# Four gate or up pieces at a time, a shared bank for the eighth chunk, and 8 KB runs of down weights

## The chip, the cores and the metric

The kernel runs on one core of a Trainium2 chip. The metric is the time of one execution on the device, in microseconds (us); the median of three runs stands for a kernel. The profile is of one execution. In its rows PE is TensorE's matmuls, PEld its loads of weights, DVE is VectorE, ACT ScalarE, POOL GpSimd, and SPq the queue of SyncE, which issues nearly all DMAs.

## The reference

One encoder block on 528 tokens (16 meta tokens and 512 inputs) of width 1024: RMSNorm, an input projection, differential attention beside a gated short convolution, an output projection, and then a layer of 16 experts, after which the meta tokens are dropped and a last RMSNorm follows. The experts are what this change touches. Each expert picks the 66 tokens with the highest affinity to it:

```
aff = softmax(hs @ w_router)                 # hs: normed hidden state, 528 x 1024
g, idx = top_k(aff.T, 66)                    # per expert
xg = hs[idx]                                 # 16 x 66 x 1024
a = xg @ w_gate ; u = xg @ w_up              # 66 x 2048 for each expert
y = (silu(a) * u) @ w_down                   # 66 x 1024
out = zeros.at[idx].add(y * g)               # back to the tokens
```

All weights are float32, 8 MB each for gate, up and down of one expert, so that the layer reads 402.7 MB (384 MiB) of them.

## The kernel before

The experts' weights come in pieces of 1 MiB. A gate or up piece has 256 of the 1024 input rows (two blocks of 128) and 1024 of the 2048 hidden columns; there are 16 of them for an expert: for each half h of the hidden columns four of gate (into the bank tile G) and then four of up (into U). A down piece has 256 of the 2048 hidden rows and all 1024 columns; there are 8. All go into one ring of 20 buffers (`raw`). The list `tasks` holds them in the order of use, `pump` (L752) issues a DMA on SyncE's queue for the next of them as soon as the ring's next buffer is free, and `nextw` pumps and hands the oldest piece to the matmuls.

The program of the expert layer is written out by hand in one loop over the experts (`manual_schedule`), and each engine runs its part in that order. For expert e TensorE does:

- a gate or up piece: 32 products (`prod`, L941) of a 128x64 block of weights, loaded, with the 66 gathered tokens X as what moves; float32 makes two matmuls and two loads of each, so a piece has 64 matmuls and 64 loads in the trace;
- after every second such piece, the one-hot product of the expert e-2 (`to_tokens`, L998: 128 tokens by 512 columns, two matmuls into the bank T, added into `acc` by VectorE, L999), and then one down piece of the expert e-1 (`down_piece`, L968 and L970: 24 matmuls of 32 columns into `y`);
- twice an expert, four transposes for the next expert's X (`turn_x`, L953, into T as well).

After four pieces of a half, ScalarE takes Silu of G into H, or VectorE multiplies H by U. `down_rows` reads y at the end of an expert. [...] Expert 0 has gate and up pieces alone, and expert 1 no one-hot products. The last expert's eight down pieces are used in a loop of their own behind the layer (tile `ys`), and there the work is followed by the sums, the last norm and the output.

Of the kernel before, what the change touches and what calls it, by code (L numbers as in the profile page):

```python
# [10 lines left out]
F32 = mybir.dt.float32  # L11
# [8 lines left out]
P = 128  # L20
D = 1024
DC = D // P
# [5 lines left out]
NE = 16  # L28
CAP = 66
# [25 lines left out]
def block_kernel(ctx: ExitStack, tc: tile.TileContext, x, meta, mix_g, w_in, conv_w, lq1, lk1, lq2,  # L55
                 lk2, sub_g, w_out, ffn_g, w_router, w_gate, w_up, w_down, fin_g, rope, out):
    nc = tc.nc
# [18 lines left out]
    def two(ap):  # L76
# [28 lines left out]
    rows = [(meta, NMETA, 0), (x[0, 0:128], 128, 16), (x[0, 128:256], 128, 144), (x[0, 256:384], 128, 272),  # L105
            (x[0, 384:496], 112, 400), (x[0, 496:512], NMETA, 512)]
# [17 lines left out]
    ident = const.tile([P, P], F32, name="ident")  # L124
# [103 lines left out]
    HS = (slice(0, HALF), slice(HALF, L))  # L228
# [353 lines left out]
    last = [Outs(0, c, None) for c in range(0, D, 256)]  # L582
# [132 lines left out]
    def moe_raw():  # L715
        i = moe_n[0] % NRAW
        moe_n[0] += 1
        for n, p in rings:
            if i < n:
                return p.tile([P, 2048], F32, name="raw", tag="raw")  # L720
            i -= n

    tasks = []
    def gate_up(e):
        return [w[0, e, k * 256:(k + 1) * 256, h * 1024:(h + 1) * 1024].rearrange("(c p) f -> p c f", p=P)
                for h in range(2) for w in (w_gate, w_up) for k in range(4)]

    def down(e):

        for d in range(8):  # L730
            rows, cols = slice(d * 256, (d + 1) * 256), slice(0, D)
            if e == NE - 1:
                rows, cols = slice(d % 4 * 512, (d % 4 + 1) * 512), slice(d // 4 * 512, (d // 4 + 1) * 512)
            yield w_down[0, e, rows, cols].rearrange("(c p) f -> p c f", p=P)


    for e in range(NE):
        dn = down(e - 1) if e else None
        for i, t in enumerate(gate_up(e)):
            tasks.append(t)  # L740
            if e and i % 2:
                tasks.append(next(dn))
    tasks.extend(down(NE - 1))
    queue = []

    def pump(n, eng=nc.sync):
        while len(queue) < n and tasks:
            t = moe_raw()
            a = tasks.pop(0)
            v = t.rearrange("p (c f) -> p c f", c=a.shape[1])  # L750
            if tasks:
                eng.dma_start(v, a)  # L752
            else:
                for k in range(2):
                    eng.dma_start(v[:, 2 * k:2 * k + 2], a[:, 2 * k:2 * k + 2])
            queue.append(t)

    pump(RING[0])


# [87 lines left out]
    for t in range(NT):  # L848
        if t % 2 == 0:
            hn2 = ring2.tile([P, 2048], F32, name="raw", tag="raw")  # L850
        n = P if t < 4 else NMETA
# [10 lines left out]
    for t in range(NT):  # L862
        n = P if t < 4 else NMETA
# [34 lines left out]
    def gather(e):  # L898
        xg = xgp.tile([CAP, D], F32, name="xg", tag="xg")
        nc.gpsimd.indirect_dma_start(out=xg, out_offset=None, in_=hn2_d,  # L900
                                     in_offset=bass.IndirectOffsetOnAxis(ap=idxT[:CAP, e:e + 1], axis=0))
        return xg

    xg = gather(0)
# [5 lines left out]
    last = const.tile([P, 2], F32, name="last")  # L910
# [14 lines left out]
    ps2 = psm.enter_context(tc.tile_pool(name="ps2", bufs=1, space=PSUM, reuse_waits="tile"))  # L925
    NF = DFF // P
    HS = [wk.tile([P, NF, CAP], F32, name=f"H{i}") for i in range(2)]
# [3 lines left out]
    def banks(tag, n):  # L931
        return ps2.tile([P, n, 512], F32, name=tag, tag=tag, bufs=1)

    def nextw():
        pump(NRAW)
        return queue.pop(0)

    def prod(out, w, c0, x, first, last):

        for q in range(2):  # L940
            nc.tensor.matmul(out[64 * q:64 * q + 64], w[:, c0 + 64 * q:c0 + 64 * q + 64], x, start=first, stop=last,  # L941
                             skip_group_check=True)

    def at(t, i):
        return t[:, i // 4, i % 4 * CAP:(i % 4 + 1) * CAP]

    def four(t, k):
        return t[:, k, :4 * CAP].rearrange("p (c n) -> p c n", n=CAP)

    def turn_x(X, xg, k):  # L950
        t = banks("T", 1)
        for i in range(4):
            nc.tensor.transpose(at(t, i), xg[:, (4 * k + i) * P:(4 * k + i + 1) * P], ident[:CAP, :CAP])  # L953
        nc.vector.tensor_tensor(X[:, 4 * k:4 * k + 4], four(t, 0),
                                gffn[:, 4 * k:4 * k + 4, None].to_broadcast([P, 4, CAP]), op=ALU.mult)

    def new_x():
        return wk.tile([P, DC, CAP], F32, name="X", tag="X", bufs=2)

    def down_piece(y, H, d):  # L960


        w = nextw()
        for r in range(3):
            ob, ci = ((0, 0), (0, 1), (1, 0))[r]
            o = ci * 1024 + ob * 512
            for g in range(3):
                nc.tensor.matmul(y[32 * g:32 * g + 32, ob], H[:, 2 * d + ci, GR[g]:GR[g] + 32], w[:, o:o + 512],  # L968
                                 start=d == 0 and r != 1, stop=d == 7 and r != 0, skip_group_check=True)
            nc.tensor.matmul(y[96:128, r], H[:, 2 * d + 1, GR[r]:GR[r] + 32], w[:, 1536:2048], start=d == 0, stop=d == 7,  # L970
                             skip_group_check=True)

    def down_rows(y, e):

        gate = at96[:96, NE + e:NE + e + 1]
        yh = wk.tile([96, D], FR, name="yh", tag="yh")
        yl = wk.tile([96, D], FR, name="yl", tag="yl")
        tmp = wk.tile([96, 512], F32, name="tmp", tag="tmp")
        a, b = slice(0, 512), slice(512, D)
        nc.scalar.activation(yh[:, a], y[:96, 0], AF.Copy, scale=gate)  # L980
        nc.vector.scalar_tensor_tensor(yl[:, a], y[:96, 0], gate, f32(yh[:, a]), op0=ALU.mult, op1=ALU.subtract)
        for g in range(3):
            gs = slice(32 * g, 32 * g + 32)
            nc.scalar.activation(tmp[gs], y[96:128, g], AF.Copy, scale=at96[gs, NE + e:NE + e + 1])
        nc.vector.scalar_tensor_tensor(tmp, y[:96, 1], gate, tmp, op0=ALU.mult, op1=ALU.add)
        nc.scalar.copy(yh[:, b], tmp)
        nc.vector.tensor_tensor(yl[:, b], tmp, f32(yh[:, b]), op=ALU.subtract)  # L987
        oh = wk.tile([96, 512], FR, name="oh", tag="oh")
        nc.gpsimd.tensor_scalar(oh, tok, at96[:96, e:e + 1], None, op0=ALU.is_equal)  # L989
        return oh, yh, yl  # L990

    def to_tokens(po, rows, d):

        oh, yh, yl = rows
        hf, t = divmod(d, 4)
        hfs = slice(hf * 512, (hf + 1) * 512)
        for n, b in enumerate((yh, yl)):
            nc.tensor.matmul(po, oh[:, t * P:(t + 1) * P], b[:, hfs], start=n == 0, stop=n == 1)  # L998
        nc.vector.tensor_tensor(acc[:, t, hfs], acc[:, t, hfs], po, op=ALU.add)  # L999
# [3 lines left out]
    X = new_x()  # L1003
    for k in range(2):
        turn_x(X, xg, k)
    xg = gather(1)
    rows = None
    for e in range(NE):
        H = HS[e % 2]
        y = banks("y", 3) if e else None  # L1010
        i = 0
        for h in range(2):
            for n in range(2):
                t = banks("GU"[n], 2)
                for k in range(4):
                    w = nextw()
                    for ci in range(2):
                        c = 2 * k + ci
                        for j in range(8):
                            prod(at(t, j), w, ci * 1024 + j * P, X[:, c], c == 0 and j % 4 == 0, c == DC - 1)  # L1020
                    if i % 2 and rows is not None:
                        to_tokens(banks("T", 1)[:, 0], rows, i // 2)
                    if i % 2 and e:
                        down_piece(y, HS[(e - 1) % 2], i // 2)
                    i += 1
                    if i in (10, 12) and e + 1 < NE:
                        if i == 10:
                            Xn = new_x()
                        turn_x(Xn, xg, i // 2 - 5)
                        if i == 12 and e + 2 < NE:  # L1030
                            xg = gather(e + 2)
                for k in range(2):
                    dst = H[:, 8 * h + 4 * k:8 * h + 4 * k + 4]
                    src = four(t, k)
                    if n == 0:
                        nc.scalar.activation(dst, src, AF.Silu)  # L1036
                    else:
                        nc.vector.tensor_tensor(dst, dst, src, op=ALU.mult)  # L1038
        if e:
            rows = down_rows(y, e - 1)  # L1040
        X = Xn
# [23 lines left out]
    for i in range(8):  # L1065
        w = nextw()
        hf, d = divmod(i, 4)
        for ci in range(4):
            f = 4 * d + ci
# [90 lines left out]
```

## Time and profile before

| | us |
|---|---|
| median of 3 runs (1379.19 to 1382.37) | 1381.4 |
| the profiled execution | 1379.79 |
| its span in the trace | 1378.0 |
| experts 0 to 15, from the first gate matmul to the last matmul of y | 978.1 (353.5 to 1331.6) |
| from there to the end of the span | 46.4 |

The span is what lies between the first and the last instruction; 1.8 us of the execution lie outside it. The profiled execution is 1.6 us under the median. [...] Some 71% of the span is the expert layer.

### The profile page before, as it was taken

The numbers are of one execution on the slowest core, as the hardware profiler recorded it, in microseconds if no ns is written. First come the engines' busy times: TensorE is split into PE (matmuls) and PEld (weight loads), VectorE is DVE, ScalarE is ACT, GpSimd is POOL, SyncE is SP. The second block draws the span as 40 slices with busy tenths as digits, with TensorE's granted clock in tenths as the row PEclk, the third lists the DMA queues.
The fourth block names the chain that finished last, engine by engine and source line by source line (L and its number), as shares of the span: only waits on it lengthen the run. The fifth ranks groups of instructions, "written<-read, shape, count | busy, mean of one in ns | idle before, by whom it ended". The sixth has DMA issues, their size and how long they took to land.

```text
span 1378.0 us, 47059 instructions
## 1 busy us (share of the span) xinstructions
PE 1256.9 (91%) x22308; PEld 927.0 (67%) x22308; DVE 393.1 (29%) x668; ACT 231.2 (17%) x431; POOL 174.9 (13%) x139
## 2 busy tenths in 40 slices
PE   7888889994679999999999999999999999999986
PEld 6677879994666666666666666666666666666654
DVE  5876776545000111112111112111111111111115
ACT  4455444322000101011010101001010101001012
POOL 2734441331100000000000000000000000000002
PEclk8999999996899999999999999999999999999998
DMA  7311211294899999999999999999999999999992
GB/s 207 92 31 31 62 32 62 93 384 167 320 352 408 396 395 407 391 407 396 406 397 404 385 391 397 393 400 388 403 382 397 400 385 404 380 405 398 407 362 94
DMA packets 142881, 434.49 MB, mean 315 GB/s; under 512 B 13200, under 2 KB 37776, under 8 KB 142688
## 3 DMA queue, kind: packets, MB, share of 16 engines
q1 hardware_dynamic: 139936, 423.49, 80.4%
q0 software_dynamic: 2752, 8.00, 1.9%
q8 instruction: 174, 2.85, 0.8%
q14 instruction: 19, 0.16, 0.0%
HBM read 427.19 MB, written 4.26 MB: 313 GB/s over the span
## 4 chain that ended last, share of the span: by engine, by line
PE 71%; DMA 12%; DVE 7%; issue 4%; ACT 3%; POOL 2%; SPq 0%; POOLq 0%; DVEq 0%; ACTq 0%
PE y L968 19%; PE G L941 16%; PE U L941 15%; DMA raw<-in_w_gate 6%; DMA raw<-in_w_up 6%; PE T L998 5%; PE pj L274 4%; PE pj L304 3%; PE ys L941 1%; ACT qsw L365 1%; PE pj L344 1%; PE sc L430 1%; PE T L953 1%; ACT p L441 1%; PE sc L792 1%
## 5 line engine op out<-in xcount | busy, mean ns | idle before, releaser
L968 PE MATMUL y<-raw,H 128*32 128x512 f32 x2160 | 337.1, 596 | 2.0 <-issue 2.0
L970 PE MATMUL y<-raw,H 128*32 128x512 f32 x720 | 332.2, 596 | 0.0
L941 PEld LDWEIGHTS U<-X,raw 128*64 128x64 f32 x8192 | 250.2, 138 | 65.0 <-issue 46.8
L941 PEld LDWEIGHTS G<-X,raw 128*64 128x64 f32 x8192 | 250.5, 139 | 58.4 <-issue 50.1
L941 PE MATMUL U<-X,raw 128*64 128x66 f32 x8192 | 263.0, 224 | 21.0 <-issue 14.9
L941 PE MATMUL G<-X,raw 128*64 128x66 f32 x8192 | 262.9, 224 | 17.4 <-issue 15.6
L999 DVE TENSOR_TENSOR acc<-acc,T 128x512 f32<-128x512 f32 x112 | 76.9, 687 | 599.1 <-PE T L998 599.1
L968 PEld LDWEIGHTS y<-raw,H 128*32 128x32 f32 x2160 | 79.6, 109 | 190.3 <-issue 175.4
L1036 ACT ACTIVATE H<-G 128x264 f32<-128x264 f32 x64 | 21.5, 388 | 591.1 <-PE G L941 591.1
L900 POOL DMA_INDIRECT xg<-hn_rows,idxT x16 | 16.3, 1017 | 694.4 <-PE T L953 674.9
L970 PEld LDWEIGHTS y<-raw,H 128*32 128x32 f32 x720 | 69.0, 109 | 1.3 <-issue 1.0
L274 PE MATMUL pj<-xh,wl 128*128 128x264 f32 x320 | 68.8, 298 | 0.0
L274 PE MATMUL pj<-xl,wh 128*128 128x264 f32 x320 | 67.7, 295 | 0.0
L274 PE MATMUL pj<-xh,wh 128*128 128x264 f32 x320 | 67.2, 293 | 0.0
L980 ACT ACTIVATE yh<-y,at 96x512 fp32r<-96x512 f32 x15 | 10.3, 684 | 281.9 <-PE y L970 281.9
L998 PE MATMUL T<-yh,oh 96*128 96x512 f32 x112 | 55.8, 499 | 1.5 <-issue 1.5
L274 PEld LDWEIGHTS pj<-xl,wh 128*128 128x128 f32 x320 | 52.4, 199 | 0.0
L274 PEld LDWEIGHTS pj<-xh,wl 128*128 128x128 f32 x320 | 52.3, 198 | 0.1
L274 PEld LDWEIGHTS pj<-xh,wh 128*128 128x128 f32 x320 | 52.2, 198 | 0.0
L989 POOL TENSOR_SCALAR oh<-tok,at 96x512 fp32r<-96x512 int16 x15 | 23.6, 1573 | 215.9 <-PE T L998 215.8
L998 PE MATMUL T<-yl,oh 96*128 96x512 f32 x112 | 44.4, 396 | 1.5 <-DVE yl L987 1.5
L1038 DVE TENSOR_TENSOR H<-H,U 128x264 f32<-128x264 f32 x64 | 24.4, 423 | 71.4 <-PE U L941 71.4
(225 smaller groups left out, 1182.2 us busy)
## 6 DMA issues: line engine op xcount, KB each, us to landing
raw<-in_w_up SPq DMA_DIRECT2D x128, 1024.0 KB, 18.4
raw<-in_w_gate SPq DMA_DIRECT2D x126, 1024.0 KB, 19.0
raw<-in_w_down SPq DMA_DIRECT2D x126, 1024.0 KB, 19.0
raw<-in_w_in SPq DMA_DIRECT2D x24, 512.0 KB, 4.7
raw<-in_w_out SPq DMA_DIRECT2D x8, 512.0 KB, 4.3
hn_rows<-raw SPq DMA_DIRECT2D x4, 512.0 KB, 3.1
raw<-in_w_gate POOLq DMA_DIRECT2D x2, 1024.0 KB, 8.9
out<-raw SPq DMA_DIRECT2D x4, 512.0 KB, 3.0
```

Of the source, the lines that this page charges most:

```text
L274: nc.tensor.matmul(o[:, hf * 512:hf * 512 + HALF], a[:, c], b[:, HS[hf]], start=c == 0 and n == 0, stop=c == DC - 1 and n == 2)
L304: nc.tensor.matmul(o[:, hf * 512:hf * 512 + HALF], a[:, k, i * P:(i + 1) * P], b[:, HS[hf]], start=k == 0 and n == 0, stop=k == 3 and n == 2)
L344: nc.tensor.matmul(o, a[:, ts], b, start=c == 0 and n == 0, stop=c == DC - 1 and n == 2)
L900: nc.gpsimd.indirect_dma_start(out=xg, out_offset=None, in_=hn2_d, in_offset=bass.IndirectOffsetOnAxis(ap=idxT[:CAP, e:e + 1], axis=0))
L941: nc.tensor.matmul(out[64 * q:64 * q + 64], w[:, c0 + 64 * q:c0 + 64 * q + 64], x, start=first, stop=last, skip_group_check=True)
L968: nc.tensor.matmul(y[32 * g:32 * g + 32, ob], H[:, 2 * d + ci, GR[g]:GR[g] + 32], w[:, o:o + 512], start=d == 0 and r != 1, stop=d == 7 an ...
L970: nc.tensor.matmul(y[96:128, r], H[:, 2 * d + 1, GR[r]:GR[r] + 32], w[:, 1536:2048], start=d == 0, stop=d == 7, skip_group_check=True)
L989: nc.gpsimd.tensor_scalar(oh, tok, at96[:96, e:e + 1], None, op0=ALU.is_equal)
L998: nc.tensor.matmul(po, oh[:, t * P:(t + 1) * P], b[:, hfs], start=n == 0, stop=n == 1)
L999: nc.vector.tensor_tensor(acc[:, t, hfs], acc[:, t, hfs], po, op=ALU.add)
L1036: nc.scalar.activation(dst, src, AF.Silu)
L1038: nc.vector.tensor_tensor(dst, dst, src, op=ALU.mult)
```

## The change

- The 16 gate and up pieces are now followed by one-hot products and down pieces after every fourth, and by two of each: four pieces, two one-hot products, two down pieces. The list of DMAs is put in the same order.
- `turn_x` comes after the eighth and twelfth piece, between the one-hot products and the down pieces.
- Of the eight chunks of 128 hidden columns in a half, seven go to one bank of G or U; the eighth goes to a bank S, which G and U share (66 columns each). So G, U and S have a bank each and T has two, in turn. Silu and the product with U are done in two instructions, of 66 and of 462 columns.
- A down piece of experts 0 to 14 is loaded so that partition p has the rows 2p and 2p+1 of its 256: 8 KB in one run instead of two of 4 KB. So that H has the same rows on the same partitions, a gate or up chunk takes every second column of a block of 256, and the weights are loaded with a step of two elements (8 bytes).
- The last expert's down pieces are taken by two rows as well (2 KB runs as before), and each is issued as two DMAs of 512 KB.

```diff
-            yield w_down[0, e, rows, cols].rearrange("(c p) f -> p c f", p=P)
+                yield w_down[0, e, rows, cols].rearrange("(b p c) f -> p b c f", p=P, c=2)
+            else:
+                yield w_down[0, e, rows, cols].rearrange("(p c) f -> p c f", p=P)
...
-            if e and i % 2:
-                tasks.append(next(dn))
+            if e and i % 4 == 3:
+                tasks += [next(dn), next(dn)]
...
-    def prod(out, w, c0, x, first, last):
+    def prod(out, w, c0, x, first, last, step=1):
 
         for q in range(2):
-            nc.tensor.matmul(out[64 * q:64 * q + 64], w[:, c0 + 64 * q:c0 + 64 * q + 64], x, start=first, stop=last,
+            c = c0 + 64 * q * step
+            nc.tensor.matmul(out[64 * q:64 * q + 64], w[:, c:c + 63 * step + 1:step], x, start=first, stop=last,
                              skip_group_check=True)
...
+    def tbank():
+        return ps2.tile([P, 512], F32, name="T", tag="T", bufs=2)
...
+            t8 = ps2.tile([P, 2, CAP], F32, name="S", tag="S", bufs=1)
             for n in range(2):
-                t = banks("GU"[n], 2)
+                t = ps2.tile([P, 512], F32, name="GU"[n], tag="GU"[n], bufs=1)
                 for k in range(4):
                     w = nextw()
                     for ci in range(2):
                         c = 2 * k + ci
                         for j in range(8):
-                            prod(at(t, j), w, ci * 1024 + j * P, X[:, c], c == 0 and j % 4 == 0, c == DC - 1)
-                    if i % 2 and rows is not None:
-                        to_tokens(banks("T", 1)[:, 0], rows, i // 2)
-                    if i % 2 and e:
-                        down_piece(y, HS[(e - 1) % 2], i // 2)
+                            prod(t[:, j * CAP:(j + 1) * CAP] if j < 7 else t8[:, n], w,
+                                 ci * 1024 + j // 2 * 256 + j % 2, X[:, c], c == 0 and j in (0, 7), c == DC - 1, 2)
                     i += 1
-                    if i in (10, 12) and e + 1 < NE:
-                        if i == 10:
+                    if i % 4:
+                        continue
+
+                    if rows is not None:
+                        for d in (i // 2 - 2, i // 2 - 1):
+                            to_tokens(tbank(), rows, d)
+                    if i in (8, 12) and e + 1 < NE:
+                        if i == 8:
                             Xn = new_x()
-                        turn_x(Xn, xg, i // 2 - 5)
+                        turn_x(Xn, xg, i // 4 - 2)
                         if i == 12 and e + 2 < NE:
                             xg = gather(e + 2)
-                for k in range(2):
-                    dst = H[:, 8 * h + 4 * k:8 * h + 4 * k + 4]
-                    src = four(t, k)
+                    if e:
+                        for d in (i // 2 - 2, i // 2 - 1):
+                            down_piece(y, HS[(e - 1) % 2], d)
+                for a, b, src in ((7, 8, t8[:, n:n + 1]), (0, 7, cols(t, 7))):
+                    dst = H[:, 8 * h + a:8 * h + b]
```

On TensorE, in the middle of an expert with one-hot products, two up pieces (64 matmuls of the program) stood ahead of one one-hot product and one down piece, whose six blocks of four matmuls begin with the last two rows:

```order
L941 MATMUL U<-X,raw 64x66 x64
L998 MATMUL T<-yh,oh 128x512
L998 MATMUL T<-yl,oh 128x512
L968 MATMUL y<-raw,H_3464 32x512 x3
L970 MATMUL y<-raw,H_3464 32x512
```

In the changed kernel a block of 128 input rows is 14 matmuls into U and 2 into S; eight such pairs of rows, of which one is shown, are the four up pieces, and two one-hot products and a turn of X follow ahead of the first of two down pieces:

```order
L944 MATMUL U<-X,raw 64x66 x14
L944 MATMUL S<-X,raw 64x66 x2
...
L1001 MATMUL T<-yh,oh 128x512
L1001 MATMUL T<-yl,oh 128x512
L1001 MATMUL T<-yh,oh 128x512
L1001 MATMUL T<-yl,oh 128x512
L956 MATMUL T<-ident,xg 128x66 x4
L971 MATMUL y<-raw,H_3463 32x512 x3
L973 MATMUL y<-raw,H_3463 32x512
```

So TensorE now has 128 program matmuls of gate or up in a row where it had 64, and what lies between is twice as long; the number of matmuls is the same.

On SyncE's queue, in the same part of the program, the weights were issued two pieces and one, all as two runs for each partition:

```order
L752 DMA raw<-in_w_up 128x2x1024 x2
L752 DMA raw<-in_w_down 128x2x1024
L752 DMA raw<-in_w_gate 128x2x1024 x2
L752 DMA raw<-in_w_down 128x2x1024
L752 DMA raw<-in_w_gate 128x2x1024 x2
```

Now they are issued four and two, and a down piece is one run of 2048 elements for each partition:

```order
L753 DMA raw<-in_w_gate 128x2x1024 x4
L753 DMA raw<-in_w_down 128x2048 x2
L753 DMA raw<-in_w_up 128x2x1024 x4
L753 DMA raw<-in_w_down 128x2048 x2
L753 DMA raw<-in_w_gate 128x2x1024 x4
```

## Rows read from the trace of the kernel before

**Rows 1.** The page: busy times and instructions, DMA queues, two groups (count, busy us, mean ns, idle before).

```profile
PE 1256.9 (91%) x22308; PEld 927.0 (67%) x22308; DVE 393.1 (29%) x668; ACT 231.2 (17%) x431; POOL 174.9 (13%) x139
...
q1 hardware_dynamic: 139936, 423.49, 80.4%
...
q8 instruction: 174, 2.85, 0.8%
...
L941 PEld LDWEIGHTS U<-X,raw 128*64 128x64 f32 x8192 | 250.2, 138 | 65.0 <-issue 46.8
...
L999 DVE TENSOR_TENSOR acc<-acc,T 128x512 f32<-128x512 f32 x112 | 76.9, 687 | 599.1 <-PE T L998 599.1
```

**Rows 2.** Experts 0, 1, 2, 11, 13, 15: us, busy (x instructions) by engine, clock, DMA.

```profile
353.50:401.50 48.00, 34.47 (x1032) 33.19 (x1033) 2.07 (x5) 2.63 (x5) 2.00 (x2) 0.96 0.99 364
401.50:461.00 59.50, 57.36 (x1233) 39.02 (x1229) 3.17 (x8) 1.34 (x4) 2.54 (x2) 0.97 1.02 391
461.00:523.90 62.90, 60.27 (x1244) 39.45 (x1240) 9.82 (x17) 4.70 (x9) 2.60 (x2) 1.00 1.03 400
...
1015.20:1076.30 61.10, 59.82 (x1244) 39.60 (x1242) 9.82 (x17) 4.70 (x9) 2.58 (x2) 1.00 1.02 397
...
1138.80:1205.00 66.20, 62.42 (x1246) 41.30 (x1242) 9.82 (x17) 4.70 (x9) 2.58 (x2) 0.97 1.02 392
...
1268.80:1331.60 62.80, 59.99 (x1236) 39.00 (x1232) 9.04 (x15) 4.69 (x9) 2.61 (x2) 1.00 1.01 390
```

**Rows 3.** TensorE in order of time in expert 0: start, length, group, [idle before].

```profile
364.78 0.74 PE L941 MATMUL G<-X,raw 128*64 128x66 f32 x18 [2.44 <-issue]
...
370.15 3.95 PE L941 MATMUL U<-X,raw 128*64 128x66 f32 x128 [1.42 <-issue]
...
393.39 3.95 PE L941 MATMUL U<-X,raw 128*64 128x66 f32 x128 [1.35 <-issue]
400.68 1.06 PE L941 MATMUL U<-X,raw 128*64 128x66 f32 x26 [3.34 <-issue]
```

**Rows 4.** TensorE in order of time in expert 4.

```profile
607.18 0.60 PE L968 MATMUL y<-raw,H 128*32 128x512 f32 x3
...
607.72 3.96 PE L941 MATMUL U<-X,raw 128*64 128x66 f32 x128
611.61 0.50 PE L998 MATMUL T<-yh,oh 96*128 96x512 f32 x1
...
612.27 0.63 PE L968 MATMUL y<-raw,H 128*32 128x512 f32 x3
...
614.98 3.84 PE L941 MATMUL G<-X,raw 128*64 128x66 f32 x124
620.08 0.34 PE L941 MATMUL G<-X,raw 128*64 128x66 f32 x4 [1.25 <-issue]
...
623.72 0.46 PE L953 MATMUL T<-ident,xg 66*128 66x66 f32 x4
624.11 3.96 PE L941 MATMUL G<-X,raw 128*64 128x66 f32 x128
```

**Rows 5.** TensorE's waits, 461 to 1015 us: total us, times, longest.

```profile
PE U L941 <- issue: 6.4, 9, 1.1
PE G L941 <- issue: 6.2, 6, 1.7
```

**Rows 6.** TensorE's longest wait in total, 1138 to 1332 us.

```profile
PE U L941 <- DMA raw<-in_w_up: 4.3, 8, 2.0
```

**Rows 7.** DMA queue 1, 100 to 250 us, then 660 to 1330 us.

```profile
q1 hardware_dynamic: 11465, 7.32, 16.5%
...
q1 hardware_dynamic: 67911, 259.66, 99.3%
```

**Rows 8.** The chain that ended last, where the expert layer ends.

```profile
1307.00 19.03 DMA raw<-in_w_up
...
1326.07 2.09 PE U L941 x64
```

More of the change, by code (lines that the diff above doesn't have):

```diff
@@ L749, in pump @@
             a = tasks.pop(0)
-            v = t.rearrange("p (c f) -> p c f", c=a.shape[1])
-            if tasks:
-                eng.dma_start(v, a)
+            if len(a.shape) == 3:
+                eng.dma_start(t.rearrange("p (c f) -> p c f", c=a.shape[1]), a)
             else:
+                v = t.rearrange("p (b c f) -> p b c f", b=2, c=2)
                 for k in range(2):
-                    eng.dma_start(v[:, 2 * k:2 * k + 2], a[:, 2 * k:2 * k + 2])
+                    eng.dma_start(v[:, k], a[:, k])
             queue.append(t)
@@ L936, in nextw, with cols @@
         return queue.pop(0)
-    def prod(out, w, c0, x, first, last):
+    def prod(out, w, c0, x, first, last, step=1):
         for q in range(2):
-            nc.tensor.matmul(out[64 * q:64 * q + 64], w[:, c0 + 64 * q:c0 + 64 * q + 64], x, start=first, stop=last,
+            c = c0 + 64 * q * step
+            nc.tensor.matmul(out[64 * q:64 * q + 64], w[:, c:c + 63 * step + 1:step], x, start=first, stop=last,
                              skip_group_check=True)
[L944 to L948, printed above, removed]
+    def cols(t, n):
+        return t[:, :n * CAP].rearrange("p (c n) -> p c n", n=CAP)
+    def tbank():
+        return ps2.tile([P, 512], F32, name="T", tag="T", bufs=2)
     def turn_x(X, xg, k):
-        t = banks("T", 1)
+        t = tbank()
         for i in range(4):
-            nc.tensor.transpose(at(t, i), xg[:, (4 * k + i) * P:(4 * k + i + 1) * P], ident[:CAP, :CAP])
-        nc.vector.tensor_tensor(X[:, 4 * k:4 * k + 4], four(t, 0),
+            nc.tensor.transpose(t[:, i * CAP:(i + 1) * CAP], xg[:, (4 * k + i) * P:(4 * k + i + 1) * P], ident[:CAP, :CAP])
+        nc.vector.tensor_tensor(X[:, 4 * k:4 * k + 4], cols(t, 4),
                                 gffn[:, 4 * k:4 * k + 4, None].to_broadcast([P, 4, CAP]), op=ALU.mult)
```

## The prediction

> **What bounds it now.** I read the page first, then stretches of single experts, then TensorE's rows in order of time, its waits, the DMA queues and the chain. The expert layer takes 978.1 of the 1378.0 us. Expert 0, with gate and up pieces alone, takes 48.0 us, expert 1 59.5; experts 2 to 11 go from 461.0 to 1076.3, 61.5 each, the last three from 1138.8 to 1331.6, 64.3 each [rows 2]. Three things stand close together there.
>
> First, TensorE's own work. From one pair of gate or up pieces to the next is 7.26 us: the pair 3.89 (607.72 to 611.61), the one-hot product 0.66, the down piece with the change back 2.71 (612.27 to 614.98). Eight such groups and two turns of X (0.39, 623.72 to 624.11) are 58.9 us an expert [rows 4].
>
> Second, TensorE's instructions. Queue 8 moves 2.85 MB in 174 packets, and TensorE runs 22308 loads and 22308 matmuls [rows 1]: 64 bytes an instruction, 16.4 KB a packet, so 256 instructions come at a time. In expert 0 TensorE stands still with nothing but "issue" to wait for, and between two such halts lie exactly 128 matmuls with their loads, 256 instructions. The seven restarts from 364.78 to 400.68, of which four stand in the rows, are 5.98 us apart in the mean, the closest shown 5.37, although 128 matmuls need 3.9 [rows 3]. Expert 0 as a whole is 2065 instructions, 8.07 packets, one every 5.95 us; expert 1 is 9.62 packets, one every 6.19 [rows 2]. I read this as a fetch of one block while the block before runs: a block takes its own work or about 6 us, whichever is longer. Later experts mostly hide it, since their groups of 308 instructions last 7.26 us and nearly every block holds part of a down piece. What they don't hide is 61.5 - 58.9 = 2.6 us an expert, and the waits for "issue" among the gate and up matmuls show it: 15 of them, 12.6 us, the longest 1.7 [rows 5]; one stands in rows 4 (1.25 us at 620.08).
>
> Third, the DMA. Its share is 1.01 to 1.03 in every expert after the first [rows 2]. It is slower than TensorE (64.3 against 61.5 us an expert), but a full ring at the start puts it ahead. Only near the end does TensorE wait for landings [rows 6], and the chain then runs through them [rows 8]. Without those waits the layer would take 48.0 + 59.5 + 14 x 61.5 = 968.5 us, 9.6 less.
>
> **Longer runs of down weights.** No row shows 8 KB packets of weights. From 100 to 250 us the queue's packets hold 638 bytes in the mean and take 16.5% x 16 x 150 us / 11465 = 34.5 ns; from 660 to 1330 us it is 3824 bytes and 156.7 ns [rows 7]. The line through both has 10 ns for each packet, however long. A down piece loses 8 of its 16 packets on each engine, 80 ns; eight pieces are 0.64 us an expert, 120 pieces 9.6 us. Bounds: nothing (the instruction packets of [rows 1] take 0.8% x 16 x 1378 / 174 = 1.01 us for 16.4 KB, no less for each byte) and 9.6. I take 9.6; DMA then needs 63.7 us an expert. The last eight pieces keep 2 KB runs; their eight extra issues lie behind transfers.
>
> **Fewer changes on TensorE.** From the start of the last block of a down piece to the next matmul is 0.54 us; the other blocks are (2.71 - 0.54) / 5 = 0.43 apart [rows 4]. So a change costs about 0.11, with the other side perhaps 0.15, and there are four fewer an expert: -0.6 us.
>
> **Shared banks.** U's eighth chunk waits for Silu of G's; the one-hot products and two down pieces (6.6 us) lie between, except in expert 0, where the halts for instructions cover it. The next half's S waits for VectorE, which first adds two products (0.69 each [rows 1]); the down pieces cover it too. `turn_x` now needs a T bank as the first of two products is still being added: the add ends about 0.1 to 0.3 us after TensorE gets there, so +0.4 us an expert. TensorE's own work: 58.9 - 0.6 + 0.4 = 58.7.
>
> **Four pieces in a row.** This is the term that decides. A round is now 512 instructions of gate or up in 7.8 us, then 104 of products and down pieces in 6.5 us: 616 instructions, 2.41 blocks. Blocks of 256 start anywhere in it; they lie wholly inside the 512 in 257 of 616 places, so one block a round has 3.9 us of work where its successor needs 6.2 (the fetch beside a full DMA queue). That is 2.3 us; blocks just over the edge add up to 0.4. [...] No row shows this directly; but a block inside gate and up work occurs now too, in one group of several, and would wait 2.3, while the longest of 15 waits is 1.7 and the mean 0.84 [rows 5]. So the reserve lies between 0.6 and 1.5; I take 0.9: 1.4 + 0.2 a round, 6.3 us an expert. TensorE then needs 65.0 us an expert. Bounds: no reserve, 2.7 a round, 69.6; every such block at the mean wait, 0.95 a round, 62.5. Two down pieces in a block (up to 8.8 us) give nothing back, as only one block is fetched ahead.
>
> **The sum.** Expert 0 has the same work, 48.0. Expert 1, without one-hot products, 59.5 + 2.5 = 62.0. Fourteen at 65.0 are 910. Together 1020, +42 against 978.1. TensorE is then slower than the DMA, so the ring stays full, the waits for landings go, and the queue is not always full; if fetches came at expert 0's 5.95 in place of 6.19, that gives back 0.24 x 4 x 14 = 13. I take half, -6. The tail behind the layer (46.4 us) is the same work. 1379.8 + 36 = 1416 for an execution like the profiled one, which lies 1.6 us under the median of its runs; I leave that.
>
> [...]
>
> **Rivals.** *The fetch stays hidden* (the faster side): the reserve grows over the long down blocks and covers the short ones. For it: the later experts lose only 2.6 us now. Against it: expert 0. It decides if the added halts are under about 0.5 us a round. TensorE would need 61 us an expert, the DMA sets the end, and its 9.6 us come off: 1370. [...] *Half of it*: 62.2 us an expert on TensorE gives 1376 to 1386, no change in the middle. *The step of 8 bytes in the loads costs time*: no load in the rows has one. A load of 64 columns (138 ns from start to end, overlapped [rows 1]) has to keep up with 30.4 ns a pair (3.89 us / 128). If each pair took 10% longer, the 1.95 us of a piece grow by 0.2, 3.1 us an expert, part of it under the halts: 1440 to 1465; at twice the time it adds up to 31 us an expert, above 1800. [...] *No reserve at all*: 69.6 us an expert, up to 1488. *Packets stay at 4 KB*, so that the run of 2048 elements does nothing: with TensorE as the bound the time is the forecast's.
>
> **Chances.** Forecast, 1386 to 1446: 0.73. Hidden fetch, 1366 to 1376: 0.11. Half: 0.05. No reserve: 0.06. Slow loads: 0.05. The range of 8 in 10 is 1374 to 1448; it leaves out most of the hidden fetch and the two high rivals. A measurement of this kernel tells 0.2% (2.8 us) from no change; faster 0.13, same 0.04, slower 0.83.
>
> **What would show it.** Right: halts for "issue" inside the runs of gate and up matmuls, about one in each round of four pieces, 1 to 2 us long, restarts at multiples of 256 instructions, 174 packets on queue 8 as before; experts 2 to 14 at 63.5 to 66.5 us with little scatter, also at the end; waits of TensorE for raw pieces gone; DMA share in the last experts at or under 1.0; about 15,360 fewer packets on queue 1; a run of 128 gate or up matmuls still 3.9 us, loads of 138 ns. Wrong: experts at 62 us with waits for landings at the end (hidden fetch); loads longer or pairs wider than 30 ns (the step); halts ahead of S or T matmuls that name VectorE or ScalarE (banks).

## The result, and the profile after

The changed kernel takes 1424.4 us (median of 4 runs, 1417.89 to 1432.38) against 1380.67 (1379.19 to 1382.37) before: a ratio of 1.0315, 95% interval 1.0278 to 1.0352. It is slower. The profiled execution took 1417.89 us, with a span of 1416.1, and is the fastest of the four: the rows below are its, and the 6.5 us from there to the median stand in no trace.

The page of the changed kernel answers to [rows 1]: busy times, DMA queues, and groups.

```profile
PE 1249.5 (88%) x22308; PEld 955.0 (67%) x22308; DVE 387.5 (27%) x668; ACT 231.2 (16%) x431; POOL 174.9 (12%) x139
...
q1 hardware_dynamic: 124688, 423.49, 78.0%
...
q8 instruction: 175, 2.87, 0.8%
...
L944 PE MATMUL U<-X,raw 128*64 128x66 f32 x7168 | 261.3, 226 | 35.3 <-issue 35.3
L944 PEld LDWEIGHTS U<-X,raw 128*64 128x64 f32 x7168 | 246.8, 140 | 63.5 <-issue 43.2
L944 PE MATMUL G<-X,raw 128*64 128x66 f32 x7168 | 259.2, 225 | 34.4 <-issue 34.3
```

TensorE runs as many matmuls and loads as before; queue 8 brings in 175 packets, one more. Queue 1 has 15,248 packets fewer for the same bytes. A load whose columns lie 8 bytes apart takes 140 ns (138 in [rows 1]). The matmuls of U and G stand idle ahead of them for 35 us each, and nearly all of that is "issue".

Experts 0, 1, 2, 11 and 15, from their first gate matmul to the next expert's, answer to [rows 2] (same columns: the last three are TensorE's clock, DMA share and GB/s):

```profile
352.10:401.40 49.30, 38.85 (x1031) 37.53 (x1033) 1.94 (x5) 2.63 (x5) 2.00 (x2) 0.88 1.00 358
401.40:465.10 63.70, 56.29 (x1233) 38.61 (x1229) 3.08 (x8) 1.34 (x4) 2.54 (x2) 0.97 1.02 390
465.10:530.60 65.50, 60.42 (x1246) 41.33 (x1242) 9.54 (x17) 4.70 (x9) 2.60 (x2) 0.97 1.01 391
1048.60:1115.60 67.00, 59.24 (x1244) 40.90 (x1240) 9.46 (x17) 4.70 (x9) 2.58 (x2) 1.00 1.01 392
1308.10:1369.90 61.80, 58.37 (x1236) 41.29 (x1232) 8.69 (x15) 4.70 (x9) 3.10 (x2) 1.00 0.66 246
```

The layer goes from 352.1 to 1369.9, 1017.8 us (978.1 before), and what follows takes 46.2 (46.4 before). The whole loss lies in the layer: 1.3 us in expert 0, 4.2 in expert 1, and 2.7 in each of experts 2 to 14 (64.85 against 62.14, a thirteenth from the first gate matmul of expert 2 to that of expert 15); expert 15 is 1.0 shorter.

TensorE's waits in experts 2 to 14 (465.1 to 1308.1) answer to [rows 5, 6]: total us, times, longest.

```profile
PE U L944 <- issue: 27.6, 19, 2.4
PE G L944 <- issue: 24.2, 21, 2.2
PE S L944 <- issue: 8.5, 6, 1.7
PE T L956 <- DVE acc L1002: 8.4, 25, 0.8
```

No wait for a raw piece of half a us or more is left; the large ones are for instructions, in the middle of gate and up runs. In order of time, from an expert's second round on, one such halt looks like this (TensorE's timeline; the matmul ahead of the halt, the one behind it, and the next two marked waits):

```profile
682.33 0.65 PE L944 MATMUL U<-X,raw 128*64 128x66 f32 x16
684.21 0.52 PE L944 MATMUL U<-X,raw 128*64 128x66 f32 x11 [1.23 <-issue]
...
687.31 0.46 PE L956 MATMUL T<-ident,xg 66*128 66x66 f32 x4 [0.32 <-DVE acc L1002]
...
698.41 0.40 PE L944 MATMUL G<-X,raw 128*64 128x66 f32 x5 [0.65 <-issue]
```

The halt ahead of 684.21 comes between two U matmuls of one piece. The matmuls ahead of it had read from that piece already, so its data was there. What TensorE waited for is seen on DMA queue 8, which brings the instructions. From 681.6 to 682.9 us:

```profile
q8 instruction: 1, 0.02, 5.3%
```

This packet of 16 KB, 256 instructions at 64 bytes, moves from 681.68 to 682.79, and TensorE restarts 1.42 us behind it. So it is with all 60 halts of more than 0.3 us for "issue" between 353 and 1330 us of this trace: each ends 1.2 to 1.6 us after such a packet has landed, and from each restart to the next TensorE runs a multiple of 256 matmuls and loads, or 2 or 4 fewer. The packet ahead of such a halt starts 2.0 to 6.5 us after the first of the 256 instructions that TensorE runs before it halts, never earlier: one block is fetched while the block ahead of it runs.

### The profile page after: what moved, and what is told of

Its sections match the earlier page's. It is cut to its first block, busy times and chain, and to the rows that moved or that the text cites. A ratio compares the mean times of both kernels' runs of the same rounds, so it can differ in the third digit from the quotient of the medians.

```text
span 1416.1 us, 47096 instructions
## 1 busy us (share of the span) xinstructions
PE 1249.5 (88%) x22308; PEld 955.0 (67%) x22308; DVE 387.5 (27%) x668; ACT 231.2 (16%) x431; POOL 174.9 (12%) x139
## 4 chain that ended last, share of the span: by engine, by line
PE 79%; issue 8%; DVE 7%; ACT 3%; POOL 2%; DMA 1%; POOLq 0%; SPq 0%; ACTq 0%; DVEq 0%
PE y L971 22%; PE G L944 16%; PE U L944 16%; PE S L944 5%; PE pj L274 4%; PE T L1001 4%; PE pj L304 3%; PE ys L944 1%; DVE acc L1002 1%; PE pj L344 1%; PE T L956 1%; ACT qsw L365 1%; PE sc L430 1%; ACT p L441 1%; PE sc L794 1%
## 5 line engine op out<-in xcount | busy, mean ns | idle before, releaser
L971 PE MATMUL y<-raw,H 128*32 128x512 f32 x2160 | 323.8, 597 | 1.2 <-PE T L1001 1.2
L973 PE MATMUL y<-raw,H 128*32 128x512 f32 x720 | 322.5, 597 | 0.0
L944 PEld LDWEIGHTS U<-X,raw 128*64 128x64 f32 x7168 | 246.8, 140 | 63.5 <-issue 43.2
L944 PE MATMUL G<-X,raw 128*64 128x66 f32 x7168 | 259.2, 225 | 34.4 <-issue 34.3
L944 PEld LDWEIGHTS G<-X,raw 128*64 128x64 f32 x7168 | 244.6, 139 | 62.7 <-issue 62.3
L1002 DVE TENSOR_TENSOR acc<-acc,T 128x512 f32<-128x512 f32 x112 | 72.3, 684 | 667.8 <-PE T L1001 667.8
L971 PEld LDWEIGHTS y<-raw,H 128*32 128x32 f32 x2160 | 85.7, 110 | 194.3 <-issue 165.9
L944 PE MATMUL S<-X,raw 128*64 128x66 f32 x2048 | 160.8, 225 | 12.0 <-issue 11.9
L944 PEld LDWEIGHTS S<-X,raw 128*64 128x64 f32 x2048 | 115.9, 140 | 13.2 <-issue 12.9
L1046 ACT ACTIVATE H<-S 128x66 f32<-128x66 f32 x32 | 7.2, 226 | 572.0 <-PE S L944 572.0
L973 PEld LDWEIGHTS y<-raw,H 128*32 128x32 f32 x720 | 74.4, 110 | 0.0
L1001 PE MATMUL T<-yh,oh 96*128 96x512 f32 x112 | 50.2, 448 | 0.0
```

The lines of the kernel that those rows point to most:

```text
L944: nc.tensor.matmul(out[64 * q:64 * q + 64], w[:, c:c + 63 * step + 1:step], x, start=first, stop=last, skip_group_check=True)
```

## The experiments

**Two halves of the change.** The first run keeps the layout, the step, the shared bank and the product banks, and puts the order back:

```
-            if e and i % 4 == 3:
-                tasks += [next(dn), next(dn)]
+            if e and i % 2:
+                tasks.append(next(dn))
...
+                    if i % 2 and rows is not None:
+                        to_tokens(tbank(), rows, i // 2)
+                    if i % 2 and e:
+                        down_piece(y, HS[(e - 1) % 2], i // 2)
```

> The changed kernel with only its order put back (two pieces, one product, one down piece in turn, transfers in the same order); the 8 KB runs, the columns two apart, the shared eighth bank and the two banks of the products stay. Fetch theory (a block of 256 TensorE instructions takes the larger of its own work and about 6 us, and four pieces in a row make short blocks): the halts fall back to those of before, the loads with a step cost nothing, and the 8 KB runs can give up to 9.6 us: 1371 (1368 to 1380). Rival (the step, the shared bank or the larger runs cost the time, not the order): stays above 1400.

Measured: 1371.92 us, ratio to before 0.9941 (0.9923 to 0.996). The step and the bank cost nothing that shows. TensorE's waits in its experts 2 to 14 (460.1 to 1264.2):

```profile
PE U L944 <- issue: 7.0, 9, 1.8
PE S L944 <- issue: 4.1, 3, 1.8
PE G L944 <- issue: 3.3, 6, 0.9
PE T L1001 <- issue: 2.8, 2, 1.6
```

These are 17.2 us of "issue", where the rows of the changed kernel have 60.3. The second run is the kernel before, with the order alone (the turn of X comes behind the second down piece in it):

```
+            if e and i % 4 == 3:
+                tasks += [next(dn), next(dn)]
...
+                    if i % 4:
+                        continue
+                    for d in (i // 2 - 2, i // 2 - 1):
+                        if rows is not None:
+                            to_tokens(banks("T", 1)[:, 0], rows, d)
+                        if e:
+                            down_piece(y, HS[(e - 1) % 2], d)
```

> The kernel before with only the new order (four pieces in a row, then product, down piece, product, down piece, so that the one bank of the products is enough; transfers four and two); 4 KB runs, whole columns, two banks a gate or up tile as before. Fetch theory: the whole loss is there, 1418 to 1430, experts 2 to 14 at 64.5 to 66 us, some 140 halts. Rival (order is harmless): 1378 to 1384.

Measured: 1440.97 us, 1.044 (1.0423 to 1.0457): the order alone costs more than the whole change, and 11 us more than I had expected. TensorE's waits in its experts 2 to 14 (463.8 to 1326.3):

```profile
PE G L941 <- issue: 35.1, 25, 2.3
PE U L941 <- issue: 33.6, 21, 2.9
PE y L970 <- issue: 3.9, 4, 1.9
PE y L968 <- issue: 3.4, 4, 1.8
PE T L998 <- issue: 1.6, 1, 1.6
```

These are 77.6 us of "issue" against 62.7 in the same experts of the changed kernel (60.3 in the rows above and 2.4 ahead of T), 14.9 of the 19.5 us by which these thirteen experts are longer. Here product and down piece alternate, where the changed kernel has them in pairs; its down weights also come in 4 KB runs still. Why there are more halts isn't settled.

**Longer instructions.** One product of 128 columns in place of two of 64, so that a block of 256 instructions holds more work:

```
-        for q in range(2):
-            c = c0 + 64 * q * step
-            nc.tensor.matmul(out[64 * q:64 * q + 64], w[:, c:c + 63 * step + 1:step], x, ...)
+        nc.tensor.matmul(out, w[:, c0:c0 + 127 * step + 1:step], x, ...)
```

> The changed kernel with one load and one product of 128 columns in place of two of 64 in the gate and up products: half as many instructions there, the same multiplications. Fetch theory: a block of 256 instructions holds twice the work (7.8 us where a 128-column pair takes no more than two of 64 columns, 61 ns), so the halts go; expert 0 falls from 49.3 us to 31 to 36 and the whole to 1365 to 1380, where the DMA queue is the bound again. If the 128-column pair takes longer than 61 ns, expert 0 shows it: at 110 ns a pair 56 us. Rival (halts belong to the pieces or the banks, not to the count of instructions): expert 0 stays at 48 to 50 us with the same restarts and the whole at 1420 or more.

> The same 128-column products in the old order (the edit of the first run as well). Fetch theory: with no halts left the order no longer matters, so within 5 us of the 128-column run in the new order, and at or below the first run of this call (1365 to 1372), with expert 0 at 31 to 36 us. Rival: the two orders stay 40 us or more apart.

Measured: 1872.18 us (1.3557, 1.3535 to 1.358) and 1872.7 (1.3566, 1.3543 to 1.3588). The times that were expected failed outright, since a 128-column matmul takes 118 ns where two of 64 columns take 60 (last section); but the two orders can still be compared. Experts 0 and 2 of the first and expert 2 of the second:

```profile
352.90:463.10 110.20, 110.19 (x521) 110.19 (x521) 1.94 (x5) 2.63 (x5) 1.99 (x2) 0.50 0.50 170
559.80:647.30 87.50, 86.88 (x732) 69.49 (x728) 9.46 (x17) 4.69 (x9) 2.60 (x2) 1.00 0.87 292
```

```profile
559.80:647.30 87.50, 87.50 (x728) 68.31 (x727) 9.91 (x17) 4.70 (x9) 2.60 (x2) 1.00 0.89 291
```

No wait for "issue" is left in either, and the two orders take the same time to the tenth of a us. From 470 to 1690 us TensorE of the first waits for nothing but VectorE, 8.2 us at the turns of X. All transfers are there, and the halts and the effect of the order went together. Beside the slower products the DMA share fell to 0.87 and 0.89, too; that this alone ended the halts is unlikely, as the short instructions of the next experiment still halt at a share of 0.65.

**Half of the transfers.** In both orders, each loaded piece is used twice:

```
+    tasks[:-1] = tasks[:-1:2]
...
     def nextw():
+        if held:
+            return held.pop()
         pump(NRAW)
-        return queue.pop(0)
+        held.append(queue.pop(0))
+        return held[0]
```

> The changed kernel with every other weight transfer left out: each loaded piece is used for two pieces in a row, so half of the weights never come in and the results differ; TensorE's instructions and their order stay. It tells where the 6 us of a block come from. If they are the latency of a fetch whatever else moves (prediction: 5.95 to 6.19): experts 1 to 14 at 62 to 65 us, the halts still some 140, 1395 to 1420. If they are the wait behind a full DMA queue: blocks come in less time, the halts shrink, experts at 58.7 to 60 and expert 0 at 31 to 40, 1300 to 1345.

> The same halving of the transfers in the changed kernel with its old order. Latency whatever else moves: experts at 59.5 to 62 us, expert 0 at 47 to 49, 1355 to 1372, still 40 or more us below the four-piece order with half the transfers. Full DMA queue as the cause: both orders within 10 us of each other, 1300 to 1340.

Measured: 1354.02 us in the four-piece order (0.9817, 0.9797 to 0.9838) and 1330.38 in the old one (0.9639, 0.9621 to 0.9657). Neither expectation holds alone: the four-piece order comes out between the two ranges, and the orders come from 52 to 24 us apart, where 40 or more or 10 at most were expected. TensorE's waits in experts 2 to 14 of the four-piece order (446.9 to 1248.9), and in the old order:

```profile
PE G L950 <- issue: 16.6, 13, 1.9
PE U L950 <- issue: 10.3, 9, 1.9
PE T L962 <- DVE acc L1008: 8.2, 26, 0.3
PE S L950 <- issue: 4.9, 5, 1.8
```

```profile
PE S L950 <- issue: 0.6, 1, 0.6
PE G L950 <- issue: 0.4, 1, 0.4
```

With all transfers the waits for "issue" were 60.3 us in the rows of the four-piece order and 17.2 in those of the old one; here they are 31.8 and 1.0. So the time of a fetch isn't a fixed latency; a good part of it hangs on the weight transfers.

**Eight pieces in a row**, then four products, four down pieces and the whole turn of X, a stronger dose of the same order (the test of `i % 4` becomes one of `i % 8`, the ranges of two become four, and eight and four transfers alternate):

> The changed kernel with eight gate or up pieces in a row, then four products, four down pieces and the whole turn of x; transfers eight and four. Fetch theory (each block of gate and up alone takes 6 us for 3.9 us of work, what a block full of down work has to spare is lost): 69 to 73 us for an expert, 1480 to 1530. Rival (a halt or two at each change from pieces to down work and back): half as many rounds, so fewer halts than in the changed kernel, 1400 or less.

Measured: 1508.54 us, 1.0917 (1.0881 to 1.0953); experts 2 to 14 take 71.5 us each (471.4 to 1400.9) in the profiled execution, which is the slowest of the four (1519.17). Both as the fetch theory had it, against the rival of a halt at each change. TensorE's waits there:

```profile
PE U L944 <- issue: 76.6, 45, 3.6
PE G L944 <- issue: 29.9, 18, 3.1
PE S L944 <- issue: 12.9, 9, 2.2
```

In 53 places of this trace two halts stand one block of 256 instructions apart. From one restart to the next is 6.04 us in the mean there: 3.59 until the next packet of queue 8 starts, 1.05 for the packet, and 1.40 from its landing to the restart. The 6 us of the prediction are so measured, and most of them are a wait ahead of the packet.

**The wait for a product bank.** The turn of X behind the two down pieces:

```
+                    if e:
+                        for d in (i // 2 - 2, i // 2 - 1):
+                            down_piece(y, HS[(e - 1) % 2], d)
                     if i in (8, 12) and e + 1 < NE:
...
-                    if e:
-                        for d in (i // 2 - 2, i // 2 - 1):
-                            down_piece(y, HS[(e - 1) % 2], d)
```

> The changed kernel with the turn of the next expert's x moved behind the two down pieces, so that it finds both product banks free. The trace after shows two waits of 0.7 us between a turn's transposes in an expert where a product alone takes 0.33. If TensorE's own work sets the pace between the halts: 0.75 us for each of 15 experts, 1413 (1409 to 1419). If that wait lies in a fetch that has to be waited out anyway: 1421 to 1426.

Measured: 1427.47 us, 1.0361 (1.0322 to 1.0399); no gain, and just above the second range. Its waits in experts 2 to 14 (471.9 to 1314.8):

```profile
PE G L944 <- issue: 25.5, 19, 2.2
PE U L944 <- issue: 24.9, 18, 2.4
PE S L944 <- issue: 9.9, 6, 2.5
PE T L1001 <- issue: 3.5, 2, 1.8
PE y L971 <- issue: 1.8, 2, 1.2
```

The 8.4 us of waits for VectorE are gone, yet the thirteen experts take 842.9 us, and 843.0 in the changed kernel. Of what was saved, 2.9 us came back as waits for "issue" (from 62.7 to 65.6 us); most of the rest is that TensorE is busy longer, 775.6 against 770.6 us, and why isn't shown.

**No transfers in the layer.** Ten of the pieces that the ring holds at its start are used over and over:

```
     def nextw():
-        pump(NRAW)
-        return queue.pop(0)
+        used[0] += 1
+        return queue[10 + used[0] % 10]
```

> The changed kernel with no weight transfers in the expert layer at all: the twenty pieces loaded before it stay, ten of them are used in rotation, so all other weights are left out and the results differ; TensorE's instructions and order stay. With half the transfers the layer still had halts of 2.9 us an expert. If what is left of them is again the wait behind weight transfers, a fetch alone takes less than the 3.9 us of a block of gate and up: no halts, expert 0 at 31 to 33, experts 1 to 14 at 58.5 to 59.2, 1300 to 1315. If a fetch alone still takes longer than 3.9 us: halts stay, experts at 60.5 to 61.7, 1330 to 1350.

> The same, no weight transfers in the layer, in the changed kernel with its old order. Fetch theory: no halts in either order, so what is left is TensorE's own work, and there the old order has more changes between products and down work: experts at 59.6 to 60, 10 to 18 us slower than the four-piece order without transfers, the opposite sign of what the two orders do with their transfers. If the order costs something by itself (banks, evictions), the old order stays ahead.

Measured: 1309.29 us (0.9475, 0.9451 to 0.9499) with four pieces in a row, 1328.24 (0.962, 0.9598 to 0.9643) in the old order. The sign turns: without transfers the new order is the faster one by 19 us (10 to 18 were expected). Experts 0 and 2 of the first, then expert 2 of the second:

```profile
354.60:389.80 35.20, 34.37 (x1032) 33.95 (x1033) 1.93 (x5) 2.63 (x5) 3.66 (x3) 0.93 0.23 82
443.10:501.60 58.50, 57.87 (x1244) 40.21 (x1240) 9.46 (x17) 4.70 (x9) 2.58 (x2) 1.00 0.03 7
```

```profile
441.60:501.50 59.90, 59.90 (x1246) 40.02 (x1242) 9.81 (x17) 4.69 (x9) 2.58 (x2) 1.00 0.03 7
```

No wait for "issue" stands in either from expert 1 on. The first kernel's only waits there are 8.2 us for VectorE at the turn of X. Expert 0 was to take 31 to 33 us and takes 35.2; its clock is 0.93 there, and TensorE is idle for 0.8 us (35.20 less 34.37). In expert 0 of the changed kernel (352 to 402) the loads ahead of the shared bank S wait 0.3 us for ScalarE, a wait that the prediction had said the halts would cover.

A packet of queue 8 takes 1.10 us in the mean here and 1.07 in the changed kernel (from 360 to 1300 us), so the weight transfers don't lengthen the packet. What is left is the time until it starts. A block of 128 gate or up matmuls runs its 3.9 us without a halt here; if 1.1 go to the packet and 1.4 to what follows its landing, at most 1.4 are left ahead of it, an estimate, where the run with eight pieces has 3.59.

**Fewer packets still.** Gate and up pieces of 128 full rows, 8 KB runs like those of the down weights, in both orders:

```
-        return [w[0, e, k * 256:(k + 1) * 256, h * 1024:(h + 1) * 1024].rearrange("(c p) f -> p c f", p=P)
-                for h in range(2) for w in (w_gate, w_up) for k in range(4)]
+        return [w[0, e, k * P:(k + 1) * P].rearrange("(c p) f -> p c f", p=P) for w in (w_gate, w_up) for k in range(DC)]
```

> A version meant to beat both: the old order with the changed kernel's 8 KB down runs, and the gate and up pieces as 128 full rows of 8 KB too (two banks for a gate or up tile, one bank for the last two chunks of both). Half as many packets for gate and up, 2,048 fewer in an expert's weights of 16 pieces: at 10 ns each and sixteen engines 1.28 us an expert where the DMA queue is the bound; TensorE's own work is 59.8 us an expert (the run with half the transfers) and some halts stay. 1352 to 1366. If the price per packet is not what the 8 KB down runs gained, 1369 to 1374.

> The same full-row gate and up pieces in the changed kernel's four-piece order. Fetch theory: TensorE waits for its instructions and not for weights, so fewer packets help only by a shorter wait of a fetch: 1405 to 1426. If it was bound by the transfers after all: it gains as much as the old order does, 1395 to 1410 with experts at 63 us.

Measured: 1372.91 us (0.9947, 0.9929 to 0.9966) in the old order, 1418.69 (1.0282, 1.0251 to 1.0312) in the new one. The first range failed, and the lower gain that was named beside it came: queue 1 moves the weights in 92304 packets in place of 124816, and the time is that of the first run. From 700 to 900 us, first of the run with the old order and then of this one:

```profile
700.00:900.00 200.00, 196.92 (x4068) 131.89 (x4062) 33.62 (x58) 17.43 (x32) 9.29 (x7) 1.00 1.02 400
```

```profile
700.00:900.00 200.00, 197.50 (x4096) 132.21 (x4092) 34.10 (x56) 17.25 (x29) 9.31 (x7) 1.00 1.01 407
```

The rate rises, by 1.8%, while TensorE, 98 to 99% busy by the same rows, gets no faster. In the new order the time is in the range of the fetch theory, and the gain of 5.7 us on the changed kernel is inside the two intervals.

## Why the prediction was right

**What the order costs.** From the first gate matmul of expert 2 to that of expert 15, a thirteenth (old order: 460.1 to 1264.2, 444.1 to 1224.0 and 441.6 to 1219.4; four pieces without transfers: 443.1 to 1204.4; the others as above):

| us an expert | four pieces | two pieces (old order) | eight pieces |
|---|---|---|---|
| all transfers | 64.85 | 61.85 | 71.5 |
| half of them | 61.69 | 59.99 | |
| none | 58.56 | 59.83 | |

The last line is TensorE's own work, since nothing waits for instructions there. What is above it is the halts and what hangs on them: 6.3 us with four pieces and 2.0 with two. The forecast had 6.3 of halts an expert on 58.7 of work. That this rests on the fetch of instructions, and not on banks, loads or weights, is shown from four sides: the halts end 1.2 to 1.6 us behind the landing of an instruction packet, at multiples of its 256 instructions; the order alone brings the loss and its removal takes it away (first pair of runs); longer instructions end the halts and make the orders equal; and with the transfers gone, the same instructions in the same order run without a halt.

That 6.3 met 6.3 is luck in part. The waits for "issue" are 62.7 us in thirteen experts, 4.8 each: 49 halts in 52 rounds, 1.28 us in the mean, where the forecast had 1.4 and 0.2 a round (four times 1.6, which is 6.4). Most of the other 1.5 is that TensorE is busy longer, 770.6 us in the thirteen experts against 753.1 without transfers, 1.3 each, which the forecast did not have; in three of these experts the granted clock is 0.97. No run shows the reserve of 0.6 to 1.5 us, of which the forecast took 0.9; it was an estimate from the 15 waits of [rows 5]. The runs show halts of 1.28 us in the mean, and the longest, 2.4 us, is over the 2.3 that a block was to wait with no reserve at all.

The runs show the fetch of a block from both sides: without weight transfers it is hidden entirely, with no wait for "issue" from expert 1 on, and beside all of them 6.3 us an expert are lost with four pieces in a row. The same instructions in the same order halt or don't, by what else the sixteen DMA engines move (a share of 0.03 or of 1.01 to 1.02).

**The sum, term by term.** These are the terms of the profiled execution, for which 1416 was forecast and which took 1417.89. The median is 8.4 us above the forecast; the four executions lie 14.5 us apart, those of the kernel before 3.2, and why isn't known. Expert 0: 48.0 forecast, 49.3 measured; the granted clock was 0.88 there against 0.96 in [rows 2]. Expert 1: 62.0 and 63.7. Experts 2 to 15: 910 less 6, and 904.8 measured (465.1 to 1369.9). Tail: 46.4 and 46.2. Layer 1020 less 6, and 1017.8. The single experts scatter more than was said: experts 2 to 14 take 63.0 to 67.0 us, five of them outside 63.5 to 66.5.

**Work of the new order.** Forecast -0.6 for fewer changes and +0.4 for the bank of the turn. Without transfers the work went down by 59.83 - 58.56 = 1.27 us, where I had 0.2. Of the 58.56, waits for VectorE at the turn are 0.63 (8.2 us in thirteen experts), so the fewer changes and whatever else the order does to the work gave 1.9. That is the term that was sized wrong. With the transfers the waits for VectorE are 0.65 each, but the run with the turn moved has none of them and isn't faster. My 58.9 for the kernel before was worked out from one group of [rows 4]; whole experts of the old order without halts measure 59.8, in the layout of the change. By that the kernel before lost 1.7 in experts 2 to 11 (61.5 less 59.8), not 2.6.

**The relief for the fetch** (-6 us, because the DMA queue would not always be full) has nothing that shows it: the DMA share is 1.01 to 1.02 in experts 1 to 14 and 0.66 only in the last, where I had said at or under 1.0 in the last experts. The direction is right, as half the transfers show, but the queue was full as before. What came in its place: expert 15 at 61.8, 3.2 under the 65.0 forecast, and the other thirteen at 64.85, 2.0 in all. That these 5.2 us come near to the 6 is luck.

**Longer runs** were forecast at 9.6 us where the DMA is the bound, and at nothing in the changed kernel. In the old order the kernel with them is 8.8 us faster (1380.76 to 1371.92), and the waits for in_w_up of [rows 6] are gone. Of the 7.3 us between the two profiled executions 4.9 lie in the layer and 2.1 ahead of it; in the layer the last three experts take 185.5 us in place of 192.8, and those ahead of them 2.4 more. So the sign and the place are right, and that 8.8 is near 9.6 is luck. Nor is there a price by the packet in the time. Full rows for gate and up take away more than twice as many packets again and give nothing: once the landings are in time the old order stands at TensorE's 59.83 and the 2.0 above it. The rate follows the 10 ns roughly (395 GB/s before, 400, then 407, from 700 to 900 us).

**Rivals.** The step in the loads: 140 ns, 30 ns a matmul (rows below), and a 1371.92 us kernel that has it; it costs nothing that can be measured (a load took 138 ns before). Hidden fetch: refuted, though it is what happens without transfers. Packets: 15,248 fewer, where 15,360 were forecast.

The fastest kernel of the study that leaves no work out is the first run, the change without its order: 1371.92 us, 0.9941 of the kernel before and, by the medians, 52 us under the changed kernel. The old order with full rows, at 1372.91, can't be told from it.

## What to carry to other kernels

Where TensorE runs hundreds of short loads and matmuls on end, count its instructions in units of what one packet of the instruction queue brings (256 here), and ask how long each unit runs: beside the weight transfers a unit of 3.9 us halted here, where one block followed another in 6.04 us (eight pieces in a row), and longer work elsewhere didn't pay it back: 64.85 us an expert with four pieces, 61.85 in the old order. So mix short instructions with long ones evenly; grouping like with like saved 1.27 us an expert in work and cost 4.3 in halts and what hangs on them. And a wait that was taken away ahead of another one bought nothing here: first find which wait ends last.

## What was not expected of the hardware

The fetch of instructions is slowed by the weight transfers: with four pieces the halts and what hangs on them cost 6.3, 3.1 and 0 us an expert at DMA shares of about 1.01, 0.65 and 0.03.

Two matmuls of 64 columns took half the time of one of 128, 60 against 118 ns. Both groups below are at a granted clock of 1.00: of the kernel without transfers, 32 matmuls of 64 columns (28 of G, 4 of S) in 621.69 - 620.73 = 0.96 us, 30 ns each; then of the kernel with 128 columns, 16 matmuls (14 and 2) in 1003.05 - 1001.16 = 1.89 us, 118 ns each.

```profile
620.73 1.01 PE L946 MATMUL G<-X,raw 128*64 128x66 f32 x28
...
621.69 1.01 PE L946 MATMUL G<-X,raw 128*64 128x66 f32 x28
```

```profile
1001.16 1.81 PE L942 MATMUL G<-X,raw 128*128 128x66 f32 x14
...
1003.05 1.81 PE L942 MATMUL G<-X,raw 128*128 128x66 f32 x14
```

A lower clock followed one long halt. In the kernel with eight pieces in a row TensorE stands still for 3.05 us up to 661.36; ahead of it the granted clock was 1.00, behind it 0.50 for at least 2.6 us, and then 1.00 again (windows; the third number from the end is the clock):

```profile
655.00:658.00 3.00, 3.00 (x108) 3.00 (x105) 0.00 (x0) 0.00 (x0) 0.00 (x0) 1.00 1.03 288
658.00:661.30 3.30, 0.31 (x11) 0.19 (x7) 0.00 (x0) 0.00 (x0) 0.00 (x0) 0.97 1.00 386
661.40:664.00 2.60, 2.60 (x49) 2.60 (x50) 0.00 (x0) 0.67 (x2) 0.00 (x0) 0.50 1.04 422
665.20:671.00 5.80, 4.96 (x165) 4.83 (x161) 0.00 (x0) 0.00 (x0) 0.00 (x0) 1.00 0.97 367
```

And in the 128-column kernel all of expert 0, 110.2 us of busy TensorE, ran at a granted clock of 0.50, although nothing halted there; why is open.
